# Output projection and all gate/up pairs by Strassen's block products

## The chip, the cores and the metric

The kernel runs on one core of one Trainium2 chip. The metric is device time in microseconds for one launch, the median of three runs; lower is better. TensorE is called PE here, VectorE DVE, ScalarE ACT, GpSimd POOL, and SyncE, which issues the DMAs, SP.

## What is computed

One layer of a streaming encoder trunk on 1024 frames of width 1024, all in float32. With `h = rmsnorm(x)`:

```python
z = h @ w_in                                   # 1024 -> 5632, split in nine
oa = hgrn2_mixer(qa, fa, ia, ga, ...)          # 4 heads of 128, recurrence in chunks of 64
ob = band_attention(qb, kb, vb, ...)           # 8 heads of 64, own chunk and 8 before
merged = sigmoid(gate_a) * (oa @ w_branch_a) + sigmoid(gate_b) * (ob @ w_branch_b)
x = x + merged @ w_out                         # output projection, 1024 x 1024
h2 = rmsnorm(x)
x = x + (silu(h2 @ w_ffn_gate) * (h2 @ w_ffn_up)) @ w_ffn_down   # 1024 -> 2816 -> 1024
h3 = rmsnorm(x)
x = x + sigmoid(h3 @ w_ple_gate) * (p @ w_ple_proj)              # p is 1024 x 256
```

## The kernel before

Everything lies features by tokens: a tile is 128 features by 1024 tokens, a "half" is 512 tokens, and x is eight such tiles. Each float32 operand is split in two parts, hi (a cast to the matmul's float32r) and lo (the remainder), and each product of two operands is three matmuls: hi by hi, hi by lo, lo by hi (`gemm`). A weight unit is 128 x 1024: SP loads it, ACT casts hi (L117), POOL subtracts lo (L118); four of them lie in a ring, and units are asked for two or three ahead. An operand of activations is split by ACT (cast) and DVE (remainder). Results lie in 8 banks of PSUM of 128 x 512. Working tiles of 128 x 1024 come from a pool of 32 "slots" and from a smaller pool called late.

The stages in order are: input projections and mixers (to about 527 us), `branches`, `out_proj`, `ff_acts` (the first two gate/up pairs of 128 features), `ff_pairs`, `ff_down`, `ple`.

- `branches` makes the gates and the two branch products, and adds them to `merged`, eight tiles, which it splits at the end. `down_sums` runs beside `branches` and `out_proj`: it reads w_ffn_down, forms the weight sums that Strassen's products need on DVE, and stores them in DRAM.
- `out_proj` is plain: per output tile c one weight unit, two halves of 8 x 3 matmuls, one addition to x on DVE, then the gate/up operand (`ffn_operand`) and the square for the norm.
- `ff_acts` computes the first four feature tiles of gate and up by plain products (`ff_first`, 96 matmuls for each of two turns), and beside that combines x's tiles into the operands of the block products (`combine`).
- `ff_pairs` computes the other tiles in 20 units (gate and up, two feature tiles and two halves each) by Strassen's scheme in Winograd's form: a 2 x 2 block product takes 7 products instead of 8. In `strassen` each product is 4 x 3 matmuls of 512 columns into one of three banks; weights for the next unit are formed meanwhile (`strassen_weights`: sums on DVE, casts on ACT, remainders on POOL or DVE).
- `ff_down` runs the down projection in 7 passes, one per block product, over all 11 feature pairs, with four banks per chain of products (x: A11, A12; y: S2, S3, A22; z: S1, S4), so that a bank accumulates one product on another. After each pass DVE, ACT and POOL add the banks to x.
- `ple` makes the embedding p @ w_ple_proj (`embed`, four tiles before the gate's first tile and four between its tiles) and the last gate.

What sets the order: the framework's scheduler orders each engine's instructions by program order and readiness at compile time. Calls through `self.V`, `self.A` and `self.G` (class `Pinned`), all matmuls and all DMAs of `load` and `store` are held in program order on their engine among themselves. A generator passed as `side` is advanced at fixed points between matmuls, and so says where the elementwise work of a stage stands in the queues.

Of the kernel before, what the change touches and what calls it, by code (L numbers as in the profile page):

```python
# [28 lines left out]
LATE = 8  # L29
LATE2 = 11  # L30
# [24 lines left out]
class Trunk:  # L55
# [48 lines left out]
    def unit(self):  # L104
        ap = self.worder[self.wnext]
        self.wnext += 1
# [568 lines left out]
    def branches(self):  # L675
# [19 lines left out]
        self.merged = []  # L695
# [5 lines left out]
        def branch(dd):  # L701
            (w,) = self.weights()
            for i in range(2):
                c = 2 * dd + i
                nc.scalar.activation(gb[c], gb[c], AF.Sigmoid)
                for half in range(2):
                    hs = slice(half * HALF, half * HALF + HALF)
                    ps = yield from self.feature(w, src, half, off=i * HALF)
                    nc.vector.tensor_tensor(gb[c][:, hs], ps, gb[c][:, hs], ALU.mult)
                    yield 2592  # L710
                (nc.gpsimd if dd < 3 else nc.vector).tensor_tensor(ma[c], ma[c], gb[c], ALU.add)  # L711
# [6 lines left out]
        self.merged = [self.split(m) for m in ma]  # L718

    def out_proj(self):  # L720
        nc = self.nc
        self.x, self.u, self.b1 = [], [], []
        self.xd = []
        for c in range(KC):
            x = self.slot(late=True)
            self.load(x, self.d["x"][c])
            (w,) = self.weights()
            if c:
                self.keep_x(c - 1)
            for half in range(2):  # L730
                hs = slice(half * HALF, half * HALF + HALF)
                ps = yield from self.feature(w, self.merged, half)
                nc.vector.tensor_tensor(x[:, hs], ps, x[:, hs], ALU.add)
                yield 5184
            self.x.append(x)
            self.ffn_operand(c)
            self.norm_feed(x, c == 0)
        self.keep_x(KC - 1)
        self.merged = None
# [5 lines left out]
    def keep_x(self, c):  # L745
        d = self.spill()
        self.store(d, self.x[c])
        self.xd.append(d)

    def ffn_operand(self, c):  # L750

        g = self.cols[:, C_FFN + c:C_FFN + c + 1]
        x = self.x[c]
        if c >= 4:
            self.u.append(self.split(x, g))
            return
        if c % 2 == 0:
            self.b1.append([(self.slot(F32R), self.slot(F32R)) for _ in range(2)])
        s = slice(c % 2 * HALF, c % 2 * HALF + HALF)
        for half, (hi, lo) in enumerate(self.b1[c // 2]):  # L760
# [669 lines left out]
```

## Time and profile before

| | |
|---|---|
| median of 3 runs | 1643.73 us (1643.13 to 1646.39) |
| the profiled execution | 1643.06 us, span of its instructions 1641.3 us |
| PE busy | 1610.5 us (98% of the span), 8812 matmuls |
| DVE, ACT, POOL busy | 1019.4, 580.4, 759.1 us |
| DMA | 169.72 MB, mean 103 GB/s |
| granted PE clock | 0.997 of full |

Each row of a group says line, engine, operation, tiles written and read, shape and count, then busy time, mean nanoseconds of one, and the idle time of its engine just before. Matmul records overlap, so the distance of two starts is the pitch. Line L52 is the `Pinned` helper, L79 the matmul helper.

### The profile page before, as it was taken

The page shows a single profiled execution, that of the slowest core. Times are in us where ns is not written, and L with a number is a line of the kernel's source. Part 1 is how long each engine was busy: PE and PEld are TensorE (multiplying, and loading weights), DVE is VectorE, ACT ScalarE, POOL GpSimd, SP SyncE. Part 2 cuts the span into 40 slices and gives each one's busy share as a digit, 9 for nine tenths or more (in the row PEclk, how much of TensorE's full clock was granted, in tenths as well). Part 3 has the DMA queues.
Part 4 walks back from the last instruction along what each step waited for, and adds up shares of the span by engine and source line. Part 5 has one row for each costly group of instructions (what it writes and reads, how often), then busy time and mean ns, then how long its engine had stood idle before and what let it go on. Part 6 is the DMA issues. An engine that isn't in the chain of part 4 may idle for free.

```text
span 1641.3 us, 22305 instructions
## 1 busy us (share of the span) xinstructions
PE 1610.5 (98%) x8812; PEld 1370.7 (84%) x8812; DVE 1019.4 (62%) x1611; ACT 580.4 (35%) x990; POOL 759.1 (46%) x433
## 2 busy tenths in 40 slices
PE   8999999999999999999999999999999999999998
PEld 6998888899997888888788788888888878888887
DVE  5566655488887333323542888888888745477343
ACT  5221221277777311112333322232222333364421
POOL 4432331343222122234144677777777756587420
PEclk9999999999999999999999999999999999999999
DMA  5101000101111354532241233323323385754211
GB/s 185 52 27 52 27 27 27 65 12 43 43 35 65 108 183 145 184 118 98 93 151 64 99 107 107 99 96 96 97 97 103 134 308 204 247 177 154 90 65 52
DMA packets 56984, 169.72 MB, mean 103 GB/s; under 512 B 6448, under 2 KB 7216, under 8 KB 55472
## 3 DMA queue, kind: packets, MB, share of 16 engines
q1 hardware_dynamic: 56736, 168.29, 30.0%
q8 instruction: 69, 1.13, 0.3%
q14 instruction: 35, 0.29, 0.1%
q10 hardware_dynamic: 144, 0.02, 0.0%
HBM read 128.17 MB, written 40.11 MB: 103 GB/s over the span
## 4 chain that ended last, share of the span: by engine, by line
PE 85%; DVE 4%; POOL 2%; issue 2%; ACT 1%; DMA 1%; SPq 0%; POOLq 0%; DVEq 0%; ACTq 0%
PE pm L79 82%; PE pm L82 3%; DVE s L52 2%; DVE m L52 1%; DVE s L171 1%; POOL s L711 1%; POOL wl L118 1%; DMA wr<-d 1%; DVE q L52 0%; DMA dq<-in_wq 0%; POOL s L52 0%; ACT s L170 0%; ACT wh L117 0%; POOL s L828 0%; DVE s L711 0%
## 5 line engine op out<-in xcount | busy, mean ns | idle before, releaser
L79 PE MATMUL pm<-s,wh 128*128 128x512 f32 (+1 forms) x2360 | 729.2, 390 | 7.3 <-ACT wh L117 5.1
L79 PEld LDWEIGHTS pm<-s,wh 128*128 128x128 f32 x2360 | 440.8, 188 | 99.2 <-ACT wh L117 5.1
L118 POOL TENSOR_TENSOR wl<-wr,wh 128x1024 fp32r<-128x1024 f32 (+2 forms) x118 | 290.4, 2467 | 470.9 <-ACT wh L117 467.0
L79 PE MATMUL pm<-s,wl 128*128 128x512 f32 (+1 forms) x1180 | 459.2, 389 | 2.7 <-POOL wl L118 2.6
L79 PE MATMUL pm<-s,whi 128*128 128x512 f32 x1120 | 348.5, 392 | 1.5 <-DVE t L52 1.5
L79 PEld LDWEIGHTS pm<-s,wl 128*128 128x128 f32 x1180 | 222.0, 188 | 50.4 <-POOL wl L118 4.7
L79 PE MATMUL pm<-wh,s 128*128 128x256 f32 (+1 forms) x1152 | 253.4, 305 | 0.0
L117 ACT CAST wh<-wr 128x1024 fp32r<-128x1024 f32 (+2 forms) x118 | 119.1, 1010 | 374.9 <-PE pm L79 177.9
L79 PEld LDWEIGHTS pm<-s,whi 128*128 128x128 f32 x1120 | 210.5, 188 | 48.6 <-DVE t L52 1.9
L79 PE MATMUL pm<-s,wlo 128*128 128x512 f32 x560 | 220.0, 393 | 2.1 <-POOL wlo L52 1.6
L52 DVE TENSOR_TENSOR s<-s,s 128x512 f32<-128x512 f32 (+2 forms) x124 | 164.7, 1354 | 90.6 <-ACT s L52 48.5
L79 PEld LDWEIGHTS pm<-wh,s 128*128 128x128 f32 x1152 | 192.1, 193 | 5.2
L79 PE MATMUL pm<-wl,s 128*128 128x256 f32 (+1 forms) x576 | 170.8, 297 | 0.8 <-POOL wl L118 0.8
L79 PEld LDWEIGHTS pm<-s,wlo 128*128 128x128 f32 x560 | 105.3, 188 | 26.6 <-POOL wlo L52 2.0
L79 PEld LDWEIGHTS pm<-wl,s 128*128 128x128 f32 x576 | 111.4, 193 | 3.2 <-POOL wl L118 1.0
L52 POOL TENSOR_TENSOR s<-s,sg 128x512 f32<-128x512 f32 x40 | 69.4, 1736 | 80.5 <-ACT sg L52 80.5
L52 DVE TENSOR_TENSOR t<-pm,t 128x512 f32<-128x512 f32 x100 | 68.6, 686 | 50.4 <-PE pm L79 47.1
L79 PE MATMUL pm<-s,s 128*128 128x64 f32 (+4 forms) x776 | 98.1, 267 | 1.6 <-DVE s L52 1.6
L52 ACT CAST whi<-q 128x512 fp32r<-128x512 f32 (+1 forms) x60 | 45.5, 759 | 145.5 <-DVE q L52 125.0
L79 PEld LDWEIGHTS pm<-s,s 128*128 128x128 f32 (+2 forms) x776 | 86.6, 174 | 6.5 <-PE pm L79 2.9
L521 POOL TENSOR_TENSOR m<-m,mhalf 128x4 f32<-128x4 f32 x32 | 33.2, 1038 | 112.5 <-DVE m L52 112.5
L52 POOL TENSOR_TENSOR wlo<-wr,whi 128x512 fp32r<-128x512 f32 (+1 forms) x40 | 82.4, 2069 | 4.1 <-ACT whi L52 3.4
(138 smaller groups left out, 1826.5 us busy)
## 6 DMA issues: line engine op xcount, KB each, us to landing
s<-d SPq DMA_DIRECT2D x43, 512.0 KB, 4.8
d<-s SPq DMA_DIRECT2D x77, 256.0 KB, 3.2
wr<-in_fm SPq DMA_DIRECT2D x22, 512.0 KB, 3.6
dq<-in_wq SPq DMA_DIRECT2D x11, 1024.0 KB, 4.8
d<-dq SPq DMA_DIRECT2D x44, 256.0 KB, 4.4
wr<-in_sg SPq DMA_DIRECT2D x20, 512.0 KB, 4.1
wr<-in_su SPq DMA_DIRECT2D x20, 512.0 KB, 4.3
wr<-d SPq DMA_DIRECT2D x20, 512.0 KB, 3.7
```

The source lines that it names most:

```text
L52: return lambda *a, **k: self.trunk.order(op(*a, **k), self.key)
L79: return self.order(self.nc.tensor.matmul(*a, **k))
L82: return self.order(self.nc.tensor.transpose(*a, **k))
L117: self.nc.scalar.copy(hi[:, c], raw[:, c])
L118: self.nc.gpsimd.tensor_tensor(lo[:, c], raw[:, c], f32(hi[:, c]), ALU.subtract)
L171: nc.vector.tensor_tensor(lo, src, f32(hi[:, :]), ALU.subtract)
L521: nc.gpsimd.tensor_tensor(ss, ss, self.mhalf[:, 0:4], ALU.pow)
L711: (nc.gpsimd if dd < 3 else nc.vector).tensor_tensor(ma[c], ma[c], gb[c], ALU.add)
```

## The change

1. Output projection. `passes` and `added` are what `ff_down` had in its body, now shared, and `out_proj` uses them: 7 passes over 4 feature pairs. `branch` writes the merged tiles as blocks B11, B12, B21, B22 (128 x 1024 holds two pairs), `branch_sums` forms T1 to T4 on DVE in two parts (after branch 1, and at the head of `out_proj`), and each block is split when its pass is near. `quad_sums`, which was `down_sums`, also makes the weight sums of w_out, all within `branches`.
2. Gate/up. All 11 pairs go by block products in 22 units; `ff_first` and `combine` go. The operands are made as blocks of x while the projection's later passes run (`ffn_side`) and after them (`ffn_last`).
3. Embedding. The first token half is computed between the projection and gate/up (`embeds(0)`) and stored in DRAM; the second half at the head of `ple`.

```diff
-LATE = 8
-LATE2 = 11
+LATE = 11
...
     def branches(self):
...
-                    nc.vector.tensor_tensor(gb[c][:, hs], ps, gb[c][:, hs], ALU.mult)
+                    self.V.tensor_tensor(gb[c][:, hs], ps, gb[c][:, hs], ALU.mult)
+                    kind = f"B{i + 1}{half + 1}"
+                    (nc.gpsimd if dd < 3 else self.V).tensor_tensor(
+                        self.m[kind, dd // 2][:, dd % 2 * HALF:dd % 2 * HALF + HALF], ma[c][:, hs], gb[c][:, hs], ALU.add)
                     yield 2592
-                (nc.gpsimd if dd < 3 else nc.vector).tensor_tensor(ma[c], ma[c], gb[c], ALU.add)
...
-        self.merged = [self.split(m) for m in ma]
+            if dd == 1:
+                self.branch_sums(0)
+
+    def branch_sums(self, i):
+        m, V = self.m, self.V
+        for kind in ("T2", "T1", "T4"):
+            m[kind, i] = self.slot()
+        V.tensor_tensor(m["B12", i], m["B22", i], m["B12", i], ALU.subtract)
+        m["T3", i] = m["B12", i]
+        V.tensor_tensor(m["T2", i], m["T3", i], m["B11", i], ALU.add)
+        V.tensor_tensor(m["T1", i], m["B22", i], m["T2", i], ALU.subtract)
+        V.tensor_tensor(m["T4", i], m["B21", i], m["T2", i], ALU.subtract)
...
     def out_proj(self):
+        self.branch_sums(1)
+        self.x, self.xd = [], [None] * KC
+        order = [(b, i) for _, b in self.KINDS for i in range(2)]
+        ready = []
+        def split():
+            if not order:
+                return
+            src = self.m.pop(order.pop(0))
+            hi, lo = self.slot(F32R), self.slot(F32R)
+            self.A.copy(hi, src)
+            self.V.tensor_tensor(lo, src, f32(hi[:, :]), ALU.subtract)
+            ready.append((hi, lo))
+        def operand(b, i):
+            got = ready.pop(0)
+            if len(ready) < 2:
+                split()
+            return got
+        for _ in range(2):
+            split()
+        yield from self.passes(4, operand, self.added(lambda c: self.x[c]), self.ffn_side())
...
+    def ffn_part(self, kind, k):
+        c = 2 * k + (kind in ("B11", "B12"))
+        half = kind in ("B11", "B21")
+        hs = slice(half * HALF, half * HALF + HALF)
+        if k % 2 == 0:
+            self.y[kind, k // 2] = self.slot()
+        x = self.x[c][:, hs]
+        self.A.activation(
+            self.y[kind, k // 2][:, k % 2 * HALF:k % 2 * HALF + HALF], x, AF.Copy, scale=self.cols[:, C_FFN + c:C_FFN + c + 1])
+        self.square(x, half)
+
+    def square(self, x, half):
...
+        if half in self.seen:
+            sq = self.slot(late=True)[:, :HALF]
+            self.A.activation(sq, x, AF.Square)
+            self.G.tensor_tensor(self.acc[:, hs], self.acc[:, hs], sq, ALU.add)
...
+    def ffn_side(self):
...
+        for kind in ("B22", "B11"):
+            for i in range(2):
+                self.ffn_part(kind, 2 * i)
+                yield
+                self.ffn_part(kind, 2 * i + 1)
+                self.ffn_cast(kind, i)
+                yield
+                if kind == "B22":
+                    yield
+                    self.ffn_rest(kind, i)
+                    yield
+            if kind == "B22":
+                self.embed_load(0)
+        for i in range(2):
+            self.ffn_rest("B11", i)
+            self.ffn_part("B12", 2 * i)
+            self.ffn_part("B12", 2 * i + 1)
+            yield
+            self.ffn_sum("T3", "B22", "B12", ALU.subtract, "B12", i)
+            self.ffn_sum("T2", "T3", "B11", ALU.add, "B11", i)
+            self.ffn_cast("T2", i)
+            yield
+
+    def ffn_last(self):
+        for k in range(4):
+            self.ffn_part("B21", k)
+        for i in range(2):
+            self.ffn_rest("T2", i)
+        yield
+        for i in range(2):
+            self.ffn_sum("T1", "B22", "T2", ALU.subtract, "B22", i)
+            self.ffn_cast("T1", i)
+        yield
+        for i in range(2):
+            self.ffn_rest("T1", i)
+            self.ffn_cast("T3", i)
+        yield
+        for i in range(2):
+            self.ffn_rest("T3", i)
+            self.ffn_cast("B21", i)
+        yield
+        for i in range(2):
+            self.ffn_rest("B21", i)
+            self.ffn_sum("T4", "B21", "T2", ALU.subtract, "B21", i)
+            self.ffn_cast("T4", i)
+        yield
+        for i in range(2):
+            self.ffn_rest("T4", i)
...
+    def ffn_ready(self):
...
+        self.strassen_load()
+        self.starting = [self.ffn_last(), self.strassen_weights()]
+        for _ in range(3):
+            for stream in self.starting:
+                next(stream)
+        for c in range(KC):
+            self.keep_x(c)
+        yield from self.embeds(0)
+        self.norm_sums()
+        self.norm_rows()
...
     def ff_pairs(self):
...
         self.strassen_load()
-        self.strassen_load()
-        drain(self.strassen_weights())
+        rest, first = self.starting
+        for _ in first:
+            next(rest, None)
+        drain(rest)
...
     def run(self):
...
-                    for i, _ in enumerate(chain(self.branches(), self.out_proj())):
-                        if i % 3 == 0:
-                            next(sums, None)
+                for i, _ in enumerate(self.branches()):
+                    if i % 2 == 0:
+                        next(sums, None)
```

`ffn_cast` is a cast on ACT, `ffn_rest` the remainder on DVE, `ffn_sum` a full-width sum on DVE, all pinned. `keep_x` stores x in DRAM until the down projection. In `ff_pairs` the line `rest, first = self.starting` names `ffn_last` "rest" and `strassen_weights` "first". `embeds` makes 8 tiles of one half, 6 matmuls each.

432 lines of the change are left out of this document (197 added, 235 removed).

## Prediction

> **What bounds the kernel now.** I read the page first: engine shares, the chain, then the stretches (busy time of each engine, in microseconds, over a window) around the three stages that the change touches.
>
> ```profile
> PE 1610.5 (98%) x8812; PEld 1370.7 (84%) x8812; DVE 1019.4 (62%) x1611; ACT 580.4 (35%) x990; POOL 759.1 (46%) x433
> PE 85%; DVE 4%; POOL 2%; issue 2%; ACT 1%; DMA 1%; SPq 0%; POOLq 0%; DVEq 0%; ACTq 0%
> 760.00:780.00 20.00, 20.00 (x90) 16.57 (x89) 10.43 (x11) 6.18 (x6) 11.91 (x5) 1.00 0.15 53
> 780.00:800.00 20.00, 18.40 (x80) 14.68 (x79) 12.58 (x12) 6.49 (x7) 4.37 (x2) 1.00 0.15 52
> 900.00:920.00 20.00, 20.00 (x89) 16.54 (x89) 13.87 (x13) 8.94 (x12) 12.93 (x8) 1.00 0.08 27
> 920.00:940.00 20.00, 16.43 (x69) 12.46 (x68) 19.48 (x19) 7.90 (x11) 11.13 (x7) 1.00 0.39 127
> ```
>
> The kernel is a queue of matmuls. TensorE (PE) is busy for all of a stretch except where one stage hands over to the next: 1.6 us at 780 to 800 (branches to output projection) and 3.57 us at 920 to 940 (gate/up's first pairs to the block-product pairs). So a matmul that goes is worth its full pitch, and a handover that grows costs its full growth. The pitch is read from starts, since the records overlap:
>
> ```profile
> 754.99 0.39 PE L79 MATMUL pm<-s,wl 128*128 128x512 f32 x1
> 755.67 0.39 PE L79 MATMUL pm<-s,wl 128*128 128x512 f32 x1
> ...
> 789.54 0.51 PE L79 MATMUL pm<-s,wh 128*128 128x512 f32 x1 [0.85 <-ACT s L170]
> 790.80 0.50 PE L79 MATMUL pm<-s,wh 128*128 128x512 f32 x1 [0.75 <-DVE s L171]
> ```
>
> The wl matmul is every third one: 0.68 / 3 = 0.2267 us a matmul. A record lasts 0.39, so a gap hides 0.16 us more than its idle time shows.
>
> **What goes.** Output projection: 8 x 2 x 8 x 3 = 384 matmuls become 7 products x 4 pairs x 4 x 3 = 336. Gate/up's first pair: two `ff_first` of 96 become two block units of 84, 168. The embedding keeps its 96. So 72 matmuls fewer: 72 x 0.2267 = **-16.3 us**. The two old handovers go as well: 1.6 + 3.57, and five gaps (two at 789, three at 920 to 933) x 0.16 = 0.8, together **-6.0 us**. What takes their place is the question, as the elementwise work around them grows while the matmuls that cover it shrink.
>
> **Prices of the elementwise work.**
>
> ```profile
> 761.06 1.23 DVE L171 TENSOR_TENSOR s<-s,s 128x1024 fp32r<-128x1024 f32 x1 [0.87 <-ACT s L170]
> 766.50 2.33 DVE L171 TENSOR_TENSOR s<-s,s 128x1024 fp32r<-128x1024 f32 x1 [0.87 <-ACT s L170]
> 765.34 2.40 POOL L118 TENSOR_TENSOR wl<-wr,wh 128x1024 fp32r<-128x1024 f32 x1
> 785.66 2.76 DVE L711 TENSOR_TENSOR s<-s,s 128x1024 f32<-128x1024 f32 x1
> 784.93 2.40 POOL L118 TENSOR_TENSOR wl<-wr,wh 128x1024 fp32r<-128x1024 f32 x1 [5.25 <-ACT wh L117]
> ...
> L709 DVE TENSOR_TENSOR s<-pm,s 128x512 f32<-128x512 f32 x16 | 10.8, 685 | 10.0 <-PE pm L79 10.0
> L1042 DVE TENSOR_TENSOR dq<-dq 128x512 f32<-128x512 f32 x11 | 7.6, 691 | 0.3
> L52 DVE TENSOR_TENSOR s<-s,s 128x1024 fp32r<-128x1024 f32 x35 | 71.6, 2058 | 46.9 <-ACT s L52 46.9
> L170 ACT CAST s<-s 128x1024 fp32r<-128x1024 f32 x26 | 26.2, 1046 | 37.8 <-POOL s L711 18.0 <-PE pm L79 11.1 <-DVE s L711 8.0
> L118 POOL TENSOR_TENSOR wl<-wr,wh 128x1024 fp32r<-128x1024 f32 x107 | 271.6, 2542 | 454.3 <-ACT wh L117 450.9 <-PE pm L79 2.6 <-POOL wl L118 0.8
> L786 POOL TENSOR_TENSOR s<-s,s 128x512 f32<-128x512 f32 x4 | 5.2, 1293 | 12.2 <-ACT s L784 12.2
> L1197 POOL TENSOR_TENSOR s<-s,s 128x512 f32<-128x512 f32 x14 | 24.6, 1765 | 0.4
> L52 POOL TENSOR_TENSOR s<-s,s 128x512 f32<-128x512 f32 x12 | 20.1, 1705 | 0.0
> L195 POOL TENSOR_TENSOR m<-m,mhalf 128x8 f32<-128x8 f32 x3 | 5.0, 1651 | 16.1 <-DVE m L193 16.1
> L1196 ACT ACTIVATE s<-s 128x512 f32<-128x512 f32 x14 | 8.6, 624 | 9.5 <-POOL s L1197 7.8 <-POOL s L52 1.6
> L52 ACT ACTIVATE s<-s,cols 128x512 fp32r<-128x512 f32 x18 | 12.9, 715 | 2.0 <-DMA s<-in_x 1.5 <-DVE s L52 0.5
> ```
>
> A full-width (128x1024) VectorE operation takes 1.23 us alone; begun while GpSimd is in an operation, it lasts until that one ends plus its own time: 765.34 + 2.40 = 767.74, and VectorE ends at 768.83; 784.93 + 2.40 = 787.33, and VectorE ends at 788.42. A half-width one takes 0.69. ScalarE casts 1024 in 1.05. GpSimd adds 512 in 1.29 alone and 1.7 to 1.77 among VectorE work, and makes a weight remainder in 2.40 to 2.54.
>
> **The first new wait, at the start of the output projection.** VectorE's operations made through `self.V` are chained in program order. After the last branch matmul they are: product 0.69, add into B22 0.69, the four sums of `branch_sums(1)` at full width, and only then the remainder of B11, which the second matmul of the pass needs though its source was ready long before. 1.38 + 5 x 1.23 = 7.5 us. The weight unit whose buffer comes free at that moment puts one 2.40 us remainder of GpSimd into this stretch; VectorE meets it somewhere inside, so I charge 1.5. **+9.0 us** (7.5 to 9.9). Queued behind it on PE is the whole projection.
>
> **The second new wait, projection to block units.** PE's own work from the last projection matmul to the one that first waits on VectorE is 48 embedding matmuls (10.9) and three products of 12 (8.2): 19.1 us. The fourth product adds into a bank that `u2` must have read, and `u2` stands on VectorE behind all of `ffn_last` and the first unit's weights: 4 adds from banks (2.8), 15 full-width operations (T2, T1, S2/S1, T3, B21, T4 remainders and the T1, T4 sums: 18.5), 6 half-width ones, two of them the next unit's (4.1), `u2` (0.7): 26.1. The last T4 cast is between two of them: 1.05. So 27.1 at least. GpSimd's work there is 4 square sums, A11's remainder, the power, A12's and S3's: 5.2 + 1.29 + 1.65 + 2.40 + 1.29 = 11.8; I charge half of it to VectorE, since GpSimd itself waits on ScalarE for part: 33.0. Then what VectorE still has queued when the projection's matmuls end. In the last four products (192 x 0.2267 = 43.5 us) GpSimd gets 8 weight remainders (20.3), 4 adds (6.8) and 10 square sums (17.7): 44.8, so it is full, and VectorE takes turns with it. The nearest stretch with both that full is this one, where PE loses nothing:
>
> ```profile
> 1460.00:1480.00 20.00, 20.00 (x90) 16.58 (x89) 18.01 (x11) 15.17 (x22) 18.20 (x10) 1.00 0.44 150
> ```
>
> so I take a backlog of 3 us (0 to 12, where 12 is a product and a bit). 36.0 - 19.1 = **+16.9 us** (8.0 with neither GpSimd nor backlog; 31.8 with all of both). Below 8.0 is excluded only as far as these operations are not quicker back to back. The turn of the norm (sums, power 1.65, rows) and `r` behind VectorE's queue lie inside this wait, not beside it. By the rule of the Trainium skill, SBUF — State Buffer, section Who interferes with whom, the port shared by VectorE and GpSimd is an exclusive lock; charging all 11.8 us of GpSimd for it, the sum would be 5.9 us higher; the rows above agree on the lock, and not on how often the two meet.
>
> **The clock after a wait.** PEclk is the third figure from the end.
>
> ```profile
> 165.00:167.50 2.50, 0.45 (x5) 0.27 (x3) 2.50 (x3) 1.24 (x2) 2.50 (x3) 1.00 0.00 0
> 167.50:170.00 2.50, 2.50 (x13) 2.50 (x14) 2.50 (x4) 0.96 (x2) 2.20 (x2) 0.52 0.00 0
> 170.00:172.00 2.00, 2.00 (x14) 2.00 (x14) 1.05 (x2) 0.00 (x0) 1.13 (x1) 0.75 0.00 0
> ...
> 526.00:530.50 4.50, 1.79 (x10) 1.17 (x8) 0.97 (x4) 4.46 (x8) 1.82 (x1) 1.00 0.36 115
> 530.50:534.00 3.50, 3.21 (x31) 2.62 (x31) 0.66 (x2) 1.19 (x2) 0.00 (x0) 1.00 0.01 2
> ```
>
> After the idle 2.05 us at 165 the clock is halved for a while: 2.5 x 0.48 + 2.0 x 0.25 = 1.7 us lost. After the idle 2.7 us at 527 it is not. Waits of 9 and 17 us are far longer than either; I charge 1.7 twice, **+3.4 us** (0 to 3.4). The Trainium skill, TensorE: Matmul & The Clock Gate, section What's actually happening, has the clock halved after an idle window of about 3.4 us; by it both waits pay and the 2.05 us one need not, where the row shows that it did.
>
> **What I cost at nothing.** Branches: 4 more weight pairs to combine (16 x 0.69 = 11 us of VectorE, 8 MB more on SP's queue), block adds in halves on GpSimd. The stretch 760 to 780 has VectorE and GpSimd half idle and PE full; uncovered, the additions would be 11 us. At the first branch all 32 slots are taken, so its four block adds wait until the last gate has read `u`; only GpSimd's adds queue behind it, no bank is held by them. Embedding: its loads, spills and reloads go on SP between weights that are asked for two units ahead (10.9 us in the projection); if they come late, a unit's 4 us. Before `norm_rows` in the last stage one embedding tile's 12 matmuls go, but 24 matmuls (5.4 us) remain over the power's 1.65.
>
> **The sum**, against the profiled execution's 1643.06 us (0.7 below the median, 1643.73): 1643.1 - 16.3 - 6.0 + 9.0 + 16.9 + 3.4 = **1650 us**.
>
> **Rivals.** (1) *Faster: GpSimd is out of the way.* Waits 7.5 and 8.0, clock paid once: 1643.1 - 22.3 + 15.5 + 1.7 = 1638; with VectorE's pitch of 1.14 (two starts, 781.40 and 782.54, below) for 20 full-width operations 1.8 less, and no clock loss, about 1635. For it: the stretch at 1460, full and without loss. Against: the average of 2.06 us above for full-width remainders among weight work, not 1.23.
>
> ```profile
> 781.40 1.23 DVE L711 TENSOR_TENSOR s<-s,s 128x1024 f32<-128x1024 f32 x1
> 782.54 0.68 DVE L709 TENSOR_TENSOR s<-pm,s 128x512 f32<-128x512 f32 x1
> ...
> DVE s L52 <- POOL s L52: 6.9, 2, 5.1
> ```
>
> (2) *Slower still: squares one at a time.* The late pool has 11 tiles; 8 hold x and 2 the embedding's input, so each square of `ffn_part` waits for GpSimd to add the one before: 0.62 + 1.77 = 2.4 us instead of ScalarE's own 1.3. Four times two products, on the way to the T1 and T2 casts, that is 8 x 1.1 = 9 us more before VectorE can go on: 1659. The last row above is the same shortage in the down projection, 5.1 us once. It decides once the squares' chain is longer than VectorE's list, some 10 us after the projection. (3) *It doesn't reach the path:* the matmuls saved were covered anyway. PE at 20.00 of 20 speaks against it: 1643.
>
> **Chances.** Forecast 0.48 (its own range 1645 to 1656), rival 1 0.28, rival 2 0.18, rival 3 0.06. Range 1635 to 1660: it takes in rivals 1 and 2. A measurement of this kernel tells 0.2% (3.3 us) from no change. Faster 0.28; same 0.11 (rival 3 and the edge between rival 1 and the forecast); slower 0.61.
>
> **What would show it.** The matmul count down by 72; PE idle about 9 us before the projection's second matmul, released by VectorE's remainder (`s`, in `split`); PE idle in one or two gaps after the embedding's matmuls, one before the norm rows and one before the fourth block product, released by VectorE, 17 us together; PEclk at half for some 3 us after each; GpSimd over 0.9 busy in the projection. Wrong if the embedding's matmuls run into the block units with under 8 us idle, or if PE waits inside the projection or the branches for weights.

## The result, and the profile after

The changed kernel takes 1663.93 us (median of four runs, 1661.35 to 1667.54) beside 1643.43 for the kernel before: a ratio of 1.0123, 95% interval 1.0098 to 1.0147. It is slower, as forecast, but by 20 us where 6 were forecast, and outside the range of 1635 to 1660. The profiled execution took 1661.35 us, 18.3 above the one of before.

The page of the changed kernel, engine shares and chain:

```profile
PE 1603.8 (97%) x8740; PEld 1364.0 (82%) x8740; DVE 1083.0 (65%) x1666; ACT 596.3 (36%) x1026; POOL 812.5 (49%) x465
PE 84%; DVE 4%; POOL 3%; issue 2%; ACT 1%; DMA 1%; SPq 0%; POOLq 0%; DVEq 0%; ACTq 0%
```

72 matmuls are gone, as counted, and 18 us of span were added all the same. GpSimd has 53 us more to do, VectorE 64. Where PE stands still, from the timeline of PE (the bracket is the idle time ahead of the instruction and who ended it):

```profile
794.01 0.80 PE L78 MATMUL pm<-s,wh 128*128 128x512 f32 x1 [9.55 <-DVE s L51]
885.16 0.76 PE L78 MATMUL pm<-ph,wh 128*128 128x512 f32 x1 [7.94 <-DVE s L51]
894.40 1.05 PE L78 MATMUL pm<-ones,s 128*128 128x1 f32 x8 [1.57 <-ACT s L1290]
900.28 1.44 PE L78 MATMUL pm<-eye,m 128*128 128x128 f32 x5 [2.43 <-POOL m L196]
919.56 1.22 PE L78 MATMUL pm<-s,whi 128*128 128x512 f32 x2 [6.21 <-DVE t L51]
```

The first line is the first wait of the forecast. The others are the second, in four pieces: the embedding's fifth tile (7.94; it needs a bank that the projection's last additions on VectorE must empty first), the norm's sums, its rows, and the fourth block product, which waits for `u2` (6.21). The stretches between them (busy time of PE, weight loads, VectorE, ScalarE, GpSimd; then PEclk):

```profile
784.00:794.00 10.00, 0.46 (x3) 0.04 (x1) 9.52 (x8) 1.99 (x2) 2.43 (x1) 0.64 0.02 4
827.00:872.00 45.00, 45.00 (x200) 37.25 (x199) 31.60 (x25) 26.39 (x35) 39.15 (x20) 1.00 0.32 106
872.00:920.00 48.00, 29.31 (x116) 23.87 (x115) 42.42 (x33) 29.45 (x44) 29.65 (x15) 0.79 0.51 186
```

From 827 to 872, the second half of the projection, PE loses nothing, and GpSimd is the engine with the least room: 39 of 45 us. Behind it PE has 29 us of records in 48. VectorE's timeline tells when the projection was really over for it (PE's last matmul of it starts at 871.24):

```profile
880.43 3.98 DVE L51 TENSOR_TENSOR s<-s,s 128x1024 f32<-128x1024 f32 x2 [0.66 <-ACT s L51]
884.34 2.47 DVE L51 TENSOR_TENSOR s<-pm,s 128x512 f32<-128x512 f32 x4
907.82 4.88 DVE L51 TENSOR_TENSOR s<-s,s 128x1024 fp32r<-128x1024 f32 x4 [3.44 <-PE pm L78]
918.83 0.68 DVE L51 TENSOR_TENSOR t<-pm,t 128x512 f32<-128x512 f32 x1
```

The four additions at 884.34 are those of S4, the projection's last product. They begin 12.9 us after its end (871.46): that is the backlog. From there to the end of `u2` (919.51) it takes another 35.2. At 907.82 VectorE itself waits 3.44 us for PE: B21's remainder needs a slot that A11's weights hold until the first product has run. Who waits for whom in 784 to 922 (in all, times, longest), and the groups of that window:

```profile
DVE s L51 <- ACT s L51: 25.8, 5, 11.5
ACT s L51 <- POOL s L51: 13.1, 6, 4.4
ACT wh L118 <- DMA wr<-d: 11.0, 3, 8.2
```

```profile
L51 DVE TENSOR_TENSOR s<-s,s 128x1024 fp32r<-128x1024 f32 x28 | 52.2, 1895 | 26.1 <-ACT s L51 22.7 <-PE pm L78 3.4
L51 POOL TENSOR_TENSOR s<-s,s 128x512 f32<-128x512 f32 x26 | 42.9, 1665 | 22.4 <-ACT s L51 20.5 <-DVE s L51 1.8
L119 POOL TENSOR_TENSOR wl<-wr,wh 128x1024 fp32r<-128x1024 f32 x13 | 36.8, 2836 | 14.1 <-ACT wh L118 12.6 <-issue 1.5
```

What this view suggests is a ring: VectorE waits for ScalarE's casts, ScalarE waits for GpSimd (a square's tile) and for late weight loads, and the loads wait for the two raw buffers, which are free again only when GpSimd has made the remainder. (The longest of VectorE's waits, 11.5 us, is not of the ring: ScalarE itself waits 14.0 us for PE there.) Of GpSimd's 26 half-width additions 14 are the norm's squares, 14 x 1.665 = 23 us. My theory after this view: **GpSimd's additions of squares are what the backlog is made of.** Against it: the single tile that is left for squares (the forecast's second rival), the banks that the embedding waits for, and VectorE's or ScalarE's own list.

### The profile page after: what moved, and what is told of

It is laid out like the page before. It is cut to its first block, busy times and chain, and to the rows that moved or that the text cites. A ratio compares the mean times of both kernels' runs of the same rounds, so it can differ in the third digit from the quotient of the medians.

```text
span 1659.6 us, 22430 instructions
## 1 busy us (share of the span) xinstructions
PE 1603.8 (97%) x8740; PEld 1364.0 (82%) x8740; DVE 1083.0 (65%) x1666; ACT 596.3 (36%) x1026; POOL 812.5 (49%) x465
## 4 chain that ended last, share of the span: by engine, by line
PE 84%; DVE 4%; POOL 3%; issue 2%; ACT 1%; DMA 1%; SPq 0%; POOLq 0%; DVEq 0%; ACTq 0%
PE pm L78 81%; DVE s L51 4%; PE pm L81 3%; POOL s L51 2%; POOL wl L119 1%; DMA wr<-in_dw 1%; ACT s L51 1%; DMA wr<-d 0%; DVE m L51 0%; ACT wh L118 0%; DVE t L51 0%; DMA wr<-in_pp 0%; ACT m L51 0%; ACT L51 0%; POOL m L196 0%
## 5 line engine op out<-in xcount | busy, mean ns | idle before, releaser
L78 PE MATMUL pm<-s,wh 128*128 128x512 f32 (+1 forms) x2136 | 662.3, 391 | 16.4 <-DVE s L51 9.5
L78 PEld LDWEIGHTS pm<-s,wh 128*128 128x128 f32 x2136 | 400.0, 189 | 99.8 <-DVE s L51 10.0
L78 PE MATMUL pm<-s,wl 128*128 128x512 f32 (+1 forms) x1068 | 416.8, 390 | 3.4 <-POOL wl L119 3.3
L78 PE MATMUL pm<-s,whi 128*128 128x512 f32 x1224 | 382.1, 393 | 6.2 <-DVE t L51 6.2
L51 DVE TENSOR_TENSOR s<-s,s 128x512 f32<-128x512 f32 (+3 forms) x172 | 243.9, 1444 | 126.4 <-ACT s L51 78.9
L78 PEld LDWEIGHTS pm<-s,whi 128*128 128x128 f32 x1224 | 231.0, 189 | 57.8 <-DVE t L51 6.6
L78 PE MATMUL pm<-s,wlo 128*128 128x512 f32 x612 | 240.7, 393 | 0.0
L78 PE MATMUL pm<-s,s 128*128 128x64 f32 (+5 forms) x788 | 102.3, 271 | 1.6 <-DVE s L51 1.6
L51 POOL TENSOR_TENSOR s<-s,s 128x512 f32<-128x512 f32 x52 | 85.9, 1665 | 28.0 <-ACT s L51 26.1
L51 DVE TENSOR_TENSOR s<-pm,s 128x512 f32<-128x512 f32 x75 | 50.2, 688 | 65.5 <-PE pm L78 53.2
```

The costliest lines, as they stand in the source:

```text
L51: return lambda *a, **k: self.trunk.order(op(*a, **k), self.key)
L78: return self.order(self.nc.tensor.matmul(*a, **k))
```

## The experiments

All are edits of the changed kernel, in five rounds beside the kernel before. Total times shift by a few us from one execution to the next, so each is given by its ratio to the kernel before (the changed kernel: 1.0123, interval 1.0098 to 1.0147) and by a **stretch** read from its trace, one profiled execution of each: from the projection's first matmul to the first one behind the last block unit, 554.1 us in the changed kernel (784.08 to 1338.16). The stretch leaves out what shifts ahead of it: its start lies between 782.6 and 789.9 us in these traces.

| edit | ratio, 95% interval | stretch, us |
|---|---|---|
| one half split before the sums | 1.0095 [1.0079, 1.0111] | 547.1 |
| squares into slots | 1.0114 [1.0097, 1.0131] | 552.9 |
| no squares | 1.0058 [1.0045, 1.0071] | 542.4 |
| S4's additions sooner | 1.0135 [1.0117, 1.0153] | 555.8 |
| additions on VectorE | 1.0158 [1.0142, 1.0174] | 559.5 |
| B21, T4 into unit 0 | 1.0122 [1.0107, 1.0137] | 554.7 |
| the same, and one half split first | 1.0074 [1.0061, 1.0087] | 545.3 |
| PE kept busy | 1.0115 [1.0100, 1.0129] | 549.5 |
| whole embedding | 1.0188 [1.0174, 1.0201] | 576.9 |
| ... with S4 sooner, one half first | 1.0156 [1.0142, 1.0170] | 571.7 |
| ... and B21, T4 into unit 0 | 1.0132 [1.0118, 1.0146] | 566.8 |
| four remainders less | 1.0118 [1.0104, 1.0131] | 556.3 |
| those, no squares, one half first | 0.9989 [0.9979, 0.9998] | 533.6 |
| squares, no additions | 1.0051 [1.0038, 1.0065] | 543.3 |
| additions, no squares | 1.0113 [1.0097, 1.0129] | 553.7 |
| squares and norm behind the projection | 1.0115 [1.0102, 1.0129] | 554.3 |

### Undoing an order: the first half split ahead of the second sum

```
     def out_proj(self):
-        self.branch_sums(1)
...
-        for _ in range(2):
-            split()
+        split()
+        self.branch_sums(1)
+        split()
```

> Base: the changed kernel, 1661 to 1664 us, whose projection starts after PE has been idle for 9.6 us (784.08, released by VectorE). Here the first B11 block is split before the four sums of branch_sums(1), the second after them. Theory (VectorE's pinned order makes the wait): what stands ahead of the first remainder falls from 1.38 + 4 x 1.23 + 1.23 to 1.38 + 1.23 = 2.6 us, the idle time to 2 to 3.5 us, the clock does not drop there, and the time falls by 6 to 8 us. Rival (the sums are owed anyway): the second block's remainder comes 5 us later, PE waits there instead, and the time falls by under 2 us.

The first wait became two, and PE did other matmuls between them:

```profile
792.72 0.80 PE L78 MATMUL pm<-s,wh 128*128 128x512 f32 x1 [2.42 <-DVE s L51]
800.84 0.50 PE L78 MATMUL pm<-s,wh 128*128 128x512 f32 x1 [0.96 <-DVE s L51]
918.57 1.22 PE L78 MATMUL pm<-s,whi 128*128 128x512 f32 x2 [6.33 <-DVE t L51]
```

The stretch fell by 7.0 us; the ratio fell by less, 0.0028 or 4.6 us, and its interval overlaps the changed kernel's. So the first wait was what the forecast said, the sums standing ahead of the remainder in one chained list, and most of it was only a matter of order. The wait for `u2` did not move.

### Which part of the squares? The tile, the work, ScalarE or GpSimd

```
-            sq = self.slot(late=True)[:, :HALF]
+            sq = self.slot(late=self.u is not None)[:, :HALF]
```

> Base: the changed kernel. Here the squares of ffn_part take their tile from the 32 slots, not from the late pool, which has one tile left; the GpSimd additions stay. Theory A (one tile: each square waits until GpSimd has added the one before, ScalarE idles 13 us for it and everything behind comes late): ScalarE's idle time ahead of squares goes from 13 to under 3 us, the second handover (PE's waits between the projection's end and the fourth block product, 28 us) falls by 5 to 9 us. Theory B (GpSimd's throughput: its 26 additions and 13 weight remainders fill it): the squares come earlier but their sums do not, and the handover changes by under 3 us.

1.2 us: many tiles for squares instead of one are worth next to nothing, though ScalarE no longer waits for GpSimd at all in 784 to 922 (13.1 us in the changed kernel). The forecast's second rival is not the cause. Then the squares and their additions left out together:

```
-        self.square(x, half)
+        if half not in getattr(self, 'seen', ()) or self.acc is None:
+            self.square(x, half)
```

> Base: the changed kernel. Left out: 14 of the 16 squares of the gate/up norm and their additions on GpSimd (the norm is then taken over two blocks only). It takes away 14 x 0.62 us of ScalarE and 14 x 1.29 to 1.77 us of GpSimd. Theory (the square sums delay ScalarE's casts and take VectorE's turn): S4's additions come within 3 us of the projection's end instead of 12.7, and the second handover falls from 28 to 13 to 17 us, 11 to 15 us less. Rival (VectorE's list alone sets it, its own 26 us of operations): 3 to 5 us less.

11.7 us of the stretch went; the wait for the embedding's banks was gone altogether, that for `u2` stayed (6.70 from start to start, 6.60 before). This took work off two engines. The next two runs took it off one each:

```
             self.A.activation(sq, x, AF.Square)
-            self.G.tensor_tensor(self.acc[:, hs], self.acc[:, hs], sq, ALU.add)
+            if self.u is not None:
+                self.G.tensor_tensor(self.acc[:, hs], self.acc[:, hs], sq, ALU.add)
```

> Left out: the 14 additions of squares on GpSimd in the gate/up norm (the squares themselves are still made on ScalarE, and are read by nobody; the norm is that of two blocks). In the run without squares and additions the stretch from the first wait to the end of the block units fell by 11.7 us from 554.1. Theory G (GpSimd, 39 of 45 us busy in the projection, is what ScalarE and the weight loads wait for): nearly all of it comes from the additions, so the stretch is 542 to 545. Theory S (ScalarE's in-order list, with 14 x 0.62 = 8.7 us of squares in it): 551 to 555.

```
+            if self.u is None:
+                self.G.tensor_tensor(self.acc[:, hs], self.acc[:, hs], x, ALU.add)
+                return
             sq = self.slot(late=True)[:, :HALF]
```

> Left out: 14 squares on ScalarE; GpSimd adds the unsquared halves instead, in the same 14 additions (so the norm is not the reference's). Theory G: GpSimd's work is as it was, so the stretch is 551 to 555. Theory S: 542 to 546.

Without the additions 10.8 us of the stretch went, without the squares 0.4. GpSimd it is (that a square no longer waits for its tile in the first of the two is worth no more than the 1.2 us above). Windows of the run without additions, then its two waits that are left behind the projection, its S4 additions on VectorE, and its group of half-width additions:

```profile
827.00:872.00 45.00, 45.00 (x200) 37.28 (x199) 32.31 (x30) 28.15 (x38) 30.72 (x14) 1.00 0.31 106
872.00:920.00 48.00, 37.45 (x162) 30.48 (x162) 41.44 (x38) 29.51 (x44) 18.21 (x10) 0.89 0.53 197
```

```profile
889.05 1.22 PE L78 MATMUL pm<-eye,m 128*128 128x128 f32 x4 [2.96 <-POOL m L196]
908.12 1.22 PE L78 MATMUL pm<-s,whi 128*128 128x512 f32 x2 [7.48 <-DVE t L51]
...
877.38 2.48 DVE L51 TENSOR_TENSOR s<-pm,s 128x512 f32<-128x512 f32 x4
...
L51 POOL TENSOR_TENSOR s<-s,s 128x512 f32<-128x512 f32 x12 | 18.1, 1537 | 15.4 <-ACT s L51 13.7 <-DVE s L51 1.8
```

GpSimd's load in 827 to 872 fell from 39.15 to 30.72; S4's additions begin 4.9 us after the projection's end (872.50 there) where they began 12.9 after it. VectorE is as busy as before in these windows (32.31 and 41.44 us), but with more operations in them, 30 and 38 where there were 25 and 33: they became shorter. The six full-width operations just ahead of S4's additions show it, first in the changed kernel, then in this run:

```profile
867.66 2.29 DVE L51 TENSOR_TENSOR s<-s,s 128x1024 fp32r<-128x1024 f32 x1
872.42 7.36 DVE L51 TENSOR_TENSOR s<-s,s 128x1024 f32<-128x1024 f32 x3 [2.47 <-ACT s L51]
880.43 3.98 DVE L51 TENSOR_TENSOR s<-s,s 128x1024 f32<-128x1024 f32 x2 [0.66 <-ACT s L51]
...
868.12 9.35 DVE L51 TENSOR_TENSOR s<-s,s 128x1024 fp32r<-128x1024 f32 x6
```

13.6 us of work with 3.1 of waits became 9.35 without any. VectorE's 39 operations from 808.89 (809.93 in this run) to S4's additions are the same in both; they took 75.45 us and now take 67.45. Of the 8.0 us, 6.1 are shorter operations (55.95 us busy, now 49.87) and 1.9 are shorter waits (19.57, now 17.67). So most of these 8.0 us came about because VectorE's operations take longer beside GpSimd's, and not by the ring. The ring is there too. With the additions and without the squares the same 39 operations took 74.88 us: VectorE was busy for only 51.73 of them, but waited 23.23, and ScalarE waited 7.4 us for the embedding's weights (0.9 in the changed kernel).

### VectorE's list, longer and shorter

```
-            self.G.tensor_tensor(self.acc[:, hs], self.acc[:, hs], sq, ALU.add)
+            (self.G if self.u is not None else self.V).tensor_tensor(self.acc[:, hs], self.acc[:, hs], sq, ALU.add)
```

> The additions of squares of the gate/up norm are issued on VectorE instead of GpSimd; nothing else is changed. Theory A (GpSimd, with 39.2 us of work in the 45 us of the projection, is the queue behind which the squares, the raw weight buffers and so the backlog stand): the 14 additions cost VectorE about 14 x 0.7 = 10 us, but GpSimd's part in 45 us falls by some 24 us; the way from the first wait to the third product of the first unit (135.5 us in the changed kernel) gets 2 to 8 us shorter. Theory B (VectorE's own list is what the end waits for, whoever feeds it): that way gets 5 to 10 us longer.

5.4 us longer. GpSimd was freed, but VectorE's chained list has 14 operations more, each behind a square of ScalarE. It waits for ScalarE in fifteen places of 784 to 922 where there were five, though hardly longer in all (27.7 us, 25.8 before):

```profile
L51 DVE TENSOR_TENSOR s<-s,s 128x512 f32<-128x512 f32 x17 | 16.5, 970 | 10.5 <-ACT s L51 10.3
927.83 1.22 PE L78 MATMUL pm<-s,whi 128*128 128x512 f32 x2 [11.72 <-DVE t L51]
```

I read that as proof of VectorE's list, and tested it by shortening the list:

```
         hi, lo = self.fo[kind, i]
+        if kind in ("T1", "T3"):
+            self.fo[kind, i] = hi, self.fo["T2", i][1]
+            return
```

> Left out: the four full-width remainders of T1 and T3, in whose place the products read T2's; so VectorE's list between the projection and the operand u2 is four operations shorter, and four slots are not held. Theory (VectorE's list, at 1.9 us for a full-width operation under load, sets when the embedding, the norm and the fourth block product can run): 4 x 1.9 = 7.6 us; the stretch from the first wait to the end of the block units, 554.1 us in the changed kernel, falls to 545 to 549 (a little lower if the slots count too). Rival (the list is late only because GpSimd and ScalarE feed it late): the operations leave gaps on VectorE, and the stretch falls by less than 2.

A miss for that reading: four full-width operations less on VectorE, and the stretch is 2.2 us longer, not 7.6 shorter; the ratio is the changed kernel's within its interval. The waits of that run say where they went:

```profile
DVE s L51 <- ACT s L51: 32.8, 6, 13.0
ACT s L51 <- POOL s L51: 13.1, 6, 4.4
```

VectorE waits for ScalarE 7.0 us longer than in the changed kernel (25.8), 5.5 of them behind S4's additions, and ScalarE for GpSimd as long as before. So VectorE is fed late there, and the length of its list does not set the end. The four operations stand behind S4's additions: of the backlog ahead of them, 13.1 us in this run, it says nothing.

### Moving the work

```
-        for i in range(2):
+        self.ffn_t(0)
+        yield
...
     def ffn_last(self):
+        self.ffn_t(1)
```

(`ffn_t(i)` is B12, T3 and T2 of one `i`; the second goes behind the pass.)

> Base: the changed kernel. The second half of the B12 blocks, with T3, T2 and the cast, moves from inside the last pass to after it, so that S4's additions stand on VectorE behind three fewer operations that wait for ScalarE. Theory (the end of VectorE's list before u2 sets the handover): the embedding's wait for banks (8.1 us at 876.83) falls to 0 to 3 us, but the same operations come later in the list; PE waits the more before the norm rows or the fourth product, and the time changes by under 3 us either way. Rival (the banks that S4 holds set it): the time falls by 6 to 8 us.

The wait for the embedding's bank fell from 7.94 to 1.44 us, and one of 8.08 came up before the norm's sums. Banks are not the cause; the wait shows wherever PE first needs something of the pile.

```
-        for i in range(2):
-            self.ffn_rest("B21", i)
-            self.ffn_sum("T4", "B21", "T2", ALU.subtract, "B21", i)
-            self.ffn_cast("T4", i)
...
-                keep = self.keep_acts(n // 2 - 1) if n and n % 2 == 0 else iter(())
+                keep = self.keep_acts(n // 2 - 1) if n and n % 2 == 0 else iter(()) if n else self.ffn_tail()
```

> The remainders of B21 and the sums, casts and remainders of T4 are moved behind the first operands of unit 0, as side work of its products, so that the operand u2 of the fourth block product stands ahead of six full-width operations on VectorE. Theory (the last wait, 6.6 us before the fourth block product, is the end of VectorE's list, 3.4 us of it a wait for slots that the first product frees): the wait falls to 0 to 1.5 us, the way from the first wait to the third product (135.5 us) gets 4 to 6.5 us shorter and the median 4 to 6 us lower. Rival (the list is only moved: the products of B21 and T4 come soon after, and PE waits for them there): less than 2 us of the total, with new waits of about 5 us inside unit 0.

The rival held: `u2`'s wait fell to 3.27, a new one of 1.98 stands ahead of a later product, and neither ratio nor stretch differs from the changed kernel's. With one half split first:

> Both edits: one half of the first block is split ahead of the second sum of the branch (as in the first experiment), and B21's remainders and T4 come behind the first operands of unit 0 (as in the one beside this). If the two waits are independent, their effects on the way from the first wait to the third product add: 6.8 and 4 to 6.5 us off 135.5 us, so 122 to 125 us, and a median 8 to 12 us under the changed kernel's, which is still 8 to 12 us over the kernel before. If the list is one list, of which every edit takes only the front, the second edit adds nothing: 128 to 129 us.

8.8 us off the stretch, of which 7.0 are the split order's. The way to the fourth product got 12.2 us shorter (787.21 to 910.54), as the theory of independent waits had it, but waits of 1.17 and 2.02 come up behind it.

```
+        ps = self.mm()
+        for _ in range(40):
+            self.mul(ps, self.onesr, ready[0][0][:, :HALF], start=True, stop=True)
         yield from self.passes(4, operand, self.added(lambda c: self.x[c]), self.ffn_side())
```

> 40 matmuls without use (40 x 0.2267 = 9.1 us) run into a spare bank during the first wait, before the first pass of the projection. Theory (the idle of 9.7 us halves the clock, and 1.5 us of matmul time are lost behind it): no half clock behind the first wait, the way from the first wait to the third product 0.5 to 2 us shorter, if the projection is what the backlog waits for; 0 if the backlog's engines set the end of that way. Rival (the wait itself grows, since the matmuls end late): 0.5 to 2 us longer.

The clock, in the changed kernel and then in this run:

```profile
786.00:797.00 11.00, 2.99 (x7) 2.44 (x8) 10.93 (x8) 1.99 (x2) 2.43 (x1) 0.54 0.14 48
...
784.00:794.00 10.00, 10.00 (x45) 8.09 (x44) 8.55 (x8) 2.00 (x2) 2.18 (x1) 1.00 0.03 14
794.00:800.00 6.00, 5.73 (x26) 4.41 (x25) 4.79 (x4) 0.00 (x0) 0.30 (x1) 1.00 0.27 87
```

So the idle halves the clock, and busy work prevents it. The profiled execution gained 4.6 us of stretch (counted from the first of the 40), more than the 1.5 that the half clock had cost. 3.5 of the 4.6 are a shorter backlog (9.4), for which no run here gives the reason. The ratio gained only 0.0008, with intervals that overlap: the price of the clock is not settled by it.

### Not halving the embedding

```
+                if half == 0 and c == 4:
+                    self.embed_cast()
...
-            if i == 3 * 11:
-                self.embed_load(1)
```

> The embedding is not halved: all 96 of its matmuls run between the projection and the block units, the second half of p cast there while the first half is multiplied, and none at the start of the last stage. Theory (what follows the projection is a backlog of the other engines, which any ready matmul covers): the second half covers most of the waits behind the embedding (2.0 + 0.8 + 2.8 before the norm, 6.6 before the fourth block product, less the matmul in each), at the price of one more full-width cast and remainder (1.05 and 1.2 to 1.9 us): the stretch from the first wait to the end of the block units, 554.1 us in the changed kernel, grows by 10.9 us of matmuls less 6 to 9 us of waits, so to 556 to 559, and the rest is 10.9 us shorter, less what the half had covered there, 2 to 6 us. Total 0 to 6 us under the changed kernel. Rival (the wait is for the norm or the late tiles, not for a list that runs out with time): the stretch grows by the full 10.9, and the total is 2 to 6 us over the changed kernel.

> Three edits together: one half of the first block split ahead of the second sum (6.95 us off the stretch from the first wait to the end of the block units, by itself), the second half of B12, T3 and T2 behind the pass, so that the last additions of the projection stand sooner on VectorE (8.3 us of wait ahead of the embedding's fifth tile became 1.8, and 8.5 came up ahead of the norm's sums), and the whole embedding in this place. Theory of the one list: the embedding no longer waits for banks, and its second half covers the 8.5 us, so the stretch is 554.1 - 6.95 + 10.9 - (9 to 12) = 546 to 549, and the total 8 to 14 us under the changed kernel's. Rival: the waits stand where they were in the first and the last of these runs, and the edits add nothing to one another: 2 to 7 us under it.

> The three edits of the run beside this, and B21's remainders and T4 moved into the first unit. With the first and the last of the four alone the stretch was 545.3. Theory: with 10.9 us more of ready matmuls and the move, what is left of the waits between projection and third product is under 4 us: stretch 541 to 546, total 10 to 18 us under the changed kernel's, about that of the kernel before. Rival: what is moved into the first unit is waited for there (2 to 3 us before the products of B21 and T4, as in the run with that edit alone), and the total stays where the run beside this has it.

All three missed: stretches of 577, 572 and 567, where at most 559, 549 and 546 were expected. The cast of the input's second half came late, and PE waited for it (`ph` is the cast; from the first of the three runs):

```profile
904.16 0.79 PE L78 MATMUL pm<-ph,wh 128*128 128x512 f32 x1 [11.45 <-ACT ph L51]
903.04 1.07 ACT L51 CAST ph<-s 128x1024 fp32r<-128x1024 f32 x1
```

The cast has no idle time ahead of it: ScalarE works without a gap from 895.93 to its start. So it stood in ScalarE's list behind the casts of the gate/up operands; whether a tile would have been free for it sooner is not shown. Whether ready matmuls would have covered the pile stays untested: mine were not ready.

### Is the pile the whole loss, and can it be put off?

> Left out: the four remainders of the run beside this and 14 of the 16 squares of the gate/up norm (so the norm is that of two blocks), with one half of the first block split ahead of the second sum. By themselves the last two took 11.7 and 6.95 us off the stretch. Theory (the whole of the forecast's error, and nearly all of the loss, is work of the other engines piled up behind the projection): the three add, less what is then no longer waited for: stretch 554.1 - 11.7 - 7 - 6 = 527 to 532, total about 1636 to 1643, at or under the kernel before. Rival (the loss has another part, in the products themselves or in the stages behind): the waits go, but the total stays 5 us or more over the kernel before.

The three edits shown above together (two of them leave work out). Expected 527 to 532 and 1636 to 1643; measured 533.6 and 1644.13, just over both, and a ratio of 0.9989: the loss against the kernel before is gone to within 0.2%. What the 72 matmuls save is still not won, as PE waits 2.42 and 2.36 us at the start of the projection, 2.92 before the norm's rows and 6.14 before the fourth block product. Its windows answer to those of the result:

```profile
827.00:872.00 45.00, 45.00 (x200) 37.12 (x199) 36.43 (x32) 30.07 (x39) 26.03 (x12) 1.00 0.38 129
872.00:920.00 48.00, 38.94 (x173) 32.32 (x172) 33.87 (x32) 23.68 (x35) 23.87 (x14) 0.89 0.49 176
```

Last, nothing left out, but the squares between the embedding's tiles, the norm inside unit 0, and one half split first:

```
-        self.square(x, half)
+        self.later.append((x, half))
...
             self.nc.scalar.copy(e[:, hs], ps)
+            for _ in range(2 if half == 0 else 0):
+                self.square(*self.later.pop(0))
...
-        self.norm_sums()
-        self.norm_rows()
+    def ffn_norm(self):
+        yield
+        self.norm_sums()
+        yield
+        self.norm_rows()
```

> A version of the change that leaves nothing out: one half of the first block split ahead of the second sum, the 16 squares with their 14 additions issued between the embedding's tiles instead of inside the projection, and the norm's sums and rows inside unit 0, behind its second and third product, where the wait for u2 stands. Theory G: the projection's GpSimd work falls by some 20 us there, S4's additions and the first operands come in time, and the norm's wait falls in with that of u2: the stretch is 536 to 544 and the total 10 to 17 us under the changed kernel's, close to the kernel before. Rival (the pile is only pushed on: 14 additions at 1.67 us are 23 us of GpSimd behind the embedding, and the norm comes that late): a wait of 8 to 15 us inside unit 0, and the total no more than 5 us under the changed kernel's.

```profile
827.00:872.00 45.00, 45.00 (x200) 37.12 (x199) 34.90 (x33) 30.04 (x37) 26.00 (x13) 1.00 0.38 136
898.54 1.87 PE L78 MATMUL pm<-ones,s 128*128 128x1 f32 x8 [11.24 <-POOL s L51]
903.79 1.86 PE L78 MATMUL pm<-ones,s 128*128 128x1 f32 x8 [3.39 <-POOL s L51]
```

The rival held. GpSimd is at 26 of 45 us in the projection, the embedding no longer waits for banks, and PE stands 11.24 and 3.39 us before the norm, released by GpSimd's additions, and 7.95 before the fourth block product. The stretch is the changed kernel's. The work has to be done somewhere before the first gate, and none of these runs found a place where it costs nothing. No version without omissions beat the kernel before; the best took 1656.67 us (ratio 1.0074).

## Why the prediction was wrong

Measured in the profiled executions, each from starts and less a pitch:

| step | forecast, us | measured, us |
|---|---|---|
| 72 matmuls fewer | -16.3 | 72 fewer |
| old handovers gone | -6.0 | gone |
| first wait | +9.0 (7.5 to 9.9) | +9.7 |
| second wait | +16.9 (8.0 to 31.8) | +29.1 |
| clock after them | +3.4 | 1.5 + 1.9 |
| norm's own matmuls, now inside the wait | not counted | -3.5 |
| start of the down projection | 0 | +1.8 |

The projection's first matmul starts 0.3 us later than in the kernel before (784.08 and 783.77). With that these add up to 18.5, beside 18.3 measured. That it is only 0.3 is luck: the kernel before lost 1.5 us to a half clock at 165 that the changed kernel was spared, and the changed kernel lost 2.7 to one at 528 (last section).

- **Right:** that only handovers count, the number and the place of both new waits, the first wait's mechanism and size, and that the second appears before the norm's rows and before the fourth block product, released by VectorE (with two places more that I had not named: the bank of the embedding's fifth tile and the norm's sums).
- **The step that failed is the backlog**, "so I take a backlog of 3 us (0 to 12, where 12 is a product and a bit)". It measured 12.9. I had counted GpSimd's work in the last four products, 44.8 us in 43.5, and had written "so it is full"; that was near (39.15 in 45 measured). The error was to price it by the stretch at 1460, where PE loses nothing. VectorE's operations are long there too, but it has time to spare: it stands idle 4.1 us for PE. From the kernel before, 1460 to 1480:

```profile
L52 DVE TENSOR_TENSOR s<-s,s 128x1024 fp32r<-128x1024 f32 x3 | 8.0, 2682 | 0.0
DVE s L52 <- PE pm L79: 4.1, 1, 4.1
```

  In the projection VectorE gets its casts late (25.8 us of waits for ScalarE), and what GpSimd adds to its operations comes on top. Without the additions of squares the backlog was 4.9 us, 8.0 less, 6.1 of it by shorter operations and 1.9 by shorter waits. What makes up the 4.9 was not taken apart. The whole second wait was then 16.6 (872.50 to 908.12, less 19.0 of matmuls), near the forecast's 16.9, in part by luck: a longer backlog (4.9 for 3) and a shorter list (30.7 for 33.0).
- **The list behind the backlog** was priced 33.0 us and measured 35.2. In it are two waits for PE that the forecast did not have, 0.86 and the 3.44 for slots. The other 30.9 are 3.8 above the bare 27.1: a third of GpSimd's 11.8 us, not the half that I charged. The two errors nearly cancel. The Trainium skill, SBUF — State Buffer, section Who interferes with whom, has the port pair that VectorE and GpSimd share as an exclusive lock. The traces agree in so far as the six operations above took 13.6 us beside GpSimd's additions and 9.35 without them. A full charge, weighed against the half in the forecast, would have been 38.9, farther off.
- **The norm** was put inside the wait, but its own matmuls (3.5 us on PE's path in the kernel before, read from starts) were not credited: an error of 3.5 to the other side.
- **Costed at nothing:** the embedding's loads and the branches' extra work cost nothing that PE shows. The start of the down projection did:

```profile
1369.15 0.73 PE L78 MATMUL pm<-s,wh 128*128 128x512 f32 x2 [0.88 <-ACT wh L118]
1371.58 0.50 PE L78 MATMUL pm<-s,wl 128*128 128x512 f32 x1 [1.70 <-POOL wl L119]
1378.39 0.50 PE L78 MATMUL pm<-s,wl 128*128 128x512 f32 x1 [1.07 <-POOL wl L119]
```

  where the kernel before has two such waits, 1.00 and 1.05. No run here looked for the reason.
- **Rivals:** GpSimd out of the way (1638) did not come about: without its additions alone the ratio is 1.0051, some 1652 us, and only the run with three edits comes near, at 1644. The squares' rival had its condition met (ScalarE waits for GpSimd 13.1 us in six waits) and its price wrong: with many tiles 1.2 us came back, not 9.

## What to carry to other kernels

An engine that you count as full costs something where the engine beside it has no time to spare. Before you price it by a stretch where the same load was harmless, look whether the other engine waits for PE there (VectorE did, 4.1 us at 1460) or is itself behind, as in the projection. A table of waits is not enough to see it: of the 8.0 us that GpSimd's additions cost VectorE's list, 6.1 lay in longer operations and 1.9 in waits. So compare the same operations in two runs, busy time and waits apart. To find which engine sets the pace, leave its work out one engine at a time: moving the work between engines or in time mostly moved the wait. Matmuls saved ahead of a handover may be cover lost for the engines beside; no run here tested that by itself.

## What the runs showed of the hardware

- The clock is already half while PE idles, and not only for the matmuls behind the wait: 0.54 in 786 to 797, where PE starts again at 794.01. So this wait of 9.7 us costs only 1.5 us of matmul time. The shorter idle of 3.83 in the attention cost more, 2.7 us: the 31 matmuls from 528.42 take 6.01 us, and 3.34 in the kernel before, where an idle of 3.00 stands in that place and no half clock follows.

```profile
528.42 1.33 PE L81 MATMUL pm<-eye,m 128*128 128x128 f32 x5 [3.83 <-DVE m L51]
```

- One and the same idle time can be followed by a half clock or not: behind the 2.05 us near 165 the clock is 0.50 in the kernel before (168 to 171) and 1.00 in the changed kernel.
- Two waits 8 us apart each halve it again:

```profile
882.00:889.50 7.50, 4.34 (x11) 3.45 (x12) 7.46 (x8) 3.18 (x5) 3.71 (x2) 0.54 0.49 197
896.00:906.50 10.50, 8.07 (x31) 7.46 (x32) 7.52 (x8) 10.50 (x16) 7.45 (x3) 0.51 0.54 202
```

  but there PE was waiting for VectorE's list anyway, so the matmuls slowed (1.9 and 1.4 us) lie inside the wait and are not added to it.
- A full-width VectorE operation, 1.23 us alone, averaged 1.895 over the 28 of 784 to 922, and a weight remainder on GpSimd 2.84 beside 2.40 alone: both slow down when both are full. Without GpSimd's additions of squares VectorE's twelve full-width sums of this window averaged 1.31 us, where they had averaged 1.75.
